# An overflow check behind the output's stores, ranking among the first products, and small experts flipped by transposes

## Chip, cores and metric

The kernel runs on one core of a Trainium2 chip. Its time is the device time of one execution in microseconds; the median of several runs is compared.

## What is computed

A two-layer encoder over 272 tokens (16 meta tokens and 256 of the sequence) of 1024 features. Layer 0 is a convolution module and a dense SwiGLU, layer 1 a pooling mixer and a mixture of experts; each part reads an RMS-normed stream and adds to it, and a last RMS norm follows. The change touches the mixture alone:

```python
def moe_swiglu(h, w_router, e_gate, e_up, e_down):
    logits = (h @ w_router).astype(jnp.float32)
    top_vals, top_idx = lax.top_k(logits, TOP_K)          # 2 of 8
    top_w = jax.nn.softmax(top_vals, axis=-1)
    ...
    for e in range(N_EXPERTS):
        y = y + combine[..., e:e + 1] * swiglu(h, e_gate[e], e_up[e], e_down[e])
```

Each expert's gate, up and down are 1024 x 3584, 1024 x 3584 and 3584 x 1024, all float32.

## The kernel before, in words

The dense layers and the router take the first 385 us. The stage of the experts takes the rest but for the tail. Experts are ranked by how many tokens chose them. Place 0 is expert 0; places 0 to 4 are "big" and hold up to 128 tokens, places 5 to 7 are "small" and hold up to 64. Should an expert have more tokens than its place holds, a body under an `If` (`second_groups`, L1240) computes the rest; on this data it is not entered. Before it, every engine loads the largest count from memory to a register (L1218).

**Steps.** The stage has 56 steps, each one expert and one block of 512 of its 3584 features (7 blocks). From step 7 on small steps stand among the big ones, mostly in turn. A step is three parts on TensorE: `project` for the gate into `pg` (L1155 to L1161), `project` for the up half into `pu`, and `down` for the block of the step before (L1207 to L1210), which adds into sums that stay in PSUM for 7 blocks. In the middle of the gate's project the block of the step before is flipped: its product of gate and up, tokens in partitions, is turned so that features are in partitions. For a big expert `flip` (L1173) does this by four transposes, and ACT and VectorE split the result into a high and a low half. A small expert keeps high and low halves of its 64 tokens side by side in 128 columns, so its halves have to be added as well: `flip_small` makes 16 products (L1190) with a matrix that adds them and scales by the token's norm factor (`factored_sums`), then Silu on ACT, a product (L1194) and the split.

**Weights.** They come as tiles of 1 MB on SP's queue into 15 buffers. Units of 128 x 1024 are split: ACT casts the high half (L104, `W.hi`), VectorE subtracts (L127, `W.lo`), four units ahead of TensorE. When a tile's last unit is read, the next load into its buffer is issued.

**Pieces.** All other work of VectorE and ACT in the stage stands in a list `side`. `beside` is called ten times a step (three in each `project`, four in `down`): it releases casts, takes one piece off the list, and then issues the low halves due. So a piece delays the low halves behind it, by its own time and by what it waits for.

**Start.** After the router VectorE ranks the experts (`places`, L894), reorders positions by place (`by_place`, L918), writes the tokens' factors (`of_tokens`, L927) and weights (`weights_of_tokens`, L935). SP loads the ids of the experts at each place, then the `If` stands, then four loads of the norm's gain on ACT's queue (L1308), and the loop of steps. The first pieces are the factors of expert 0, `rows_of_tokens` (L946), and for each other expert its selection matrix and a small product (`factors`, L1052).

**Sums and rows.** From step 3 on (`SUMS_FROM`) pieces add the high and low halves of the stream into `x_of` (L1336), add that to the accumulator `yacc` (L1352), multiply by the gain (L1341) and write it to memory as `x_rows` (L1342, POOL's queue), for two halves of tokens with one buffer. Each later expert's token rows are fetched from `x_rows` by an indirect DMA on POOL (L1065), one step ahead, and transposed in the up projection of the step ahead of its first. Outputs of all experts but the last are written to memory as `y_rows` and gathered at the end.

**Tail.** The last expert's output is added, the final norm is taken on ACT and VectorE, and four stores on the queues of ACT and SP end the kernel (L1493).

Of the kernel before, what the change touches and what calls it, by code (L numbers as in the profile page):

```python
# [39 lines left out]
ALONE, SUMS_FROM, QUIET = 6, 3, 3  # L40
# [15 lines left out]
class Weights:  # L56


    def __init__(self, nc, raw_pool, hi_pool, lo_pool, tiles):
# [9 lines left out]
        self.held, self.room = None, 0  # L69
# [62 lines left out]
    def read(self, i):  # L132

        self.left[i] -= 1
        if not self.left[i]:
            del self.raw[i]
            self.load(self.home[i])
# [27 lines left out]
def body(tc, xT, w_pw1, w_pw2, w_gu, w_dn, w_pool, m_gate, m_up, m_down, small, moe_g,  # L165
# [108 lines left out]
    twice = consts.tile([128, SMALL_CAP], F32)  # L274
# [619 lines left out]
    def places(scratch):  # L894

        hot, cmp = (squares_of(scratch, i, 1)[:, 0] for i in range(2))
        key, place, most = scratch[:, :NE], scratch[:, NE:NE + n_rest], scratch[:, 2 * NE:2 * NE + 1]
# [12 lines left out]
        DVE.tensor_copy(ids_i, place)  # L910
        DVE.tensor_tensor(cmp, hot, counts[:, None, 1:].to_broadcast(shape), op=OP.mult)
# [66 lines left out]
    yacc = pool(ctx, "yacc").tile([128, 2, D], F32, name="yacc")  # L978
    POOL.memset(yacc, 0.0)
# [14 lines left out]
    def gathered(ps, P, kk, width):  # L994

        for i in range(2):
            n = 0
            for x in (xth, xtl):
                for t in range(2):
# [3 lines left out]
                    n += 1  # L1003

# [11 lines left out]
    class Expert:  # L1016
# [36 lines left out]
        def factors(self):  # L1053

            ps = self.pm.tile([128, 512], F32, name="m")
            for t in range(2):
                PE.matmul(ps[:, :3], lhsT=self.P[:, t].bitcast(F32), rhs=rcq[:, t, self.q],
                          start=(t == 0), stop=(t == 1))
            DVE.tensor_copy(facts[:, self.q], ps[:, :3])
            DVE.tensor_copy(at[:, self.q:self.q + 1], ps[:, 1:2])  # L1060

        def fetch(self, rows):
            n = self.width
            self.rows = rows
            POOL.indirect_dma_start(  # L1065
                out=rows[:n], out_offset=None, in_=x_rows[:, :],
                in_offset=bass.IndirectOffsetOnAxis(ap=at[:n, self.q:self.q + 1], axis=0))
# [55 lines left out]
    with ExitStack() as cs:  # L1123
# [58 lines left out]
        def flip_small(gu, e):  # L1182
# [361 lines left out]
```

## Time and profile before

| | |
|---|---|
| median of 3 runs | 1341.68 us (1340.31 to 1342.72) |
| profiled execution, own time | 1339.14 us |
| its span | 1336.8 us |
| granted TensorE clock, mean | 0.994 |
| PE / DVE / ACT / POOL busy | 97% / 82% / 69% / 2% |
| moved by DMA | 414.21 MB, mean 310 GB/s |

The busy share of an engine is its time in work over the span. A wait is put down to the semaphore that came last; "issue" means that no semaphore shows what the engine waited for. In a timeline several like instructions can share a line with their count, and durations of pipelined instructions overlap, so that the time from start to start is what they take one after another. PEld is the loading of stationary operands, which overlaps products.

### The profile page before, as it was taken

What the parts mean: (1) busy time and instruction counts of PE and PEld (TensorE: products, weight loads), DVE (VectorE), ACT (ScalarE), POOL (GpSimd) and SP (SyncE); (2) the same over time, 40 slices, a digit from 0 to 9 for tenths busy, and PEclk for the clock granted to TensorE, in tenths of its full rate; (3) what the DMA queues carried; (4) which work ended last, traced back from release to release, by engine and by line L of the source; (5) the groups of instructions that cost most, each with busy time, mean ns of one, the idle gap of its engine ahead of it and who ended that gap; (6) DMA issues with size and microseconds to landing.
All of it is one profiled execution on the core that took longest, in us unless ns stands there. A gap on an engine that the chain in (4) does not pass through costs nothing.

```text
span 1336.8 us, 19372 instructions
## 1 busy us (share of the span) xinstructions
PE 1297.4 (97%) x6823; PEld 1055.9 (79%) x6823; DVE 1093.8 (82%) x1435; ACT 918.1 (69%) x1221; POOL 25.8 (2%) x34
## 2 busy tenths in 40 slices
PE   9999999999969899999999999999999999999996
PEld 9989999999957677777777777777777777777775
DVE  7997885666767878888788888888888887888876
ACT  6765643445545568777787777777877776877765
POOL 0000000000000100000000000000000000000010
PEclk9999999999989999999999999999999999999999
DMA  9700446425748899999999699999798999799970
GB/s 367 302 1 1 160 139 223 162 101 189 293 166 318 322 387 372 402 400 400 373 374 395 267 390 421 421 420 421 322 422 331 422 421 421 306 423 420 410 276 31
DMA packets 61783, 414.21 MB, mean 310 GB/s; under 512 B 6896, under 2 KB 8048, under 8 KB 14704
## 3 DMA queue, kind: packets, MB, share of 16 engines
q1 hardware_dynamic: 58032, 402.22, 75.8%
q0 software_dynamic: 1680, 6.03, 1.2%
q10 hardware_dynamic: 1968, 4.66, 1.0%
q8 instruction: 55, 0.90, 0.3%
q14 instruction: 48, 0.39, 0.1%
HBM read 407.90 MB, written 4.98 MB: 309 GB/s over the span
## 4 chain that ended last, share of the span: by engine, by line
PE 62%; DVE 5%; DMA 2%; issue 2%; ACT 1%; ACTq 0%; DVEq 0%
PE pg L1155 10%; PE pu L1155 10%; PE pu L1161 6%; PE pg L1161 6%; PE pyb L1207 4%; PE pyb L1210 4%; PE pyb L1209 4%; PE pg L1159 4%; PE pu L1159 4%; DVE w_lo L127 3%; PE m L1190 3%; PE pys L1207 3%; PE pys L1210 3%; DMA raw<-m_gate 2%; PE m L1173 1%
## 5 line engine op out<-in xcount | busy, mean ns | idle before, releaser
L127 DVE TENSOR_TENSOR w_lo<-raw,w_hi 128x1024 fp32r<-128x1024 f32 (+1 forms) x704 | 821.0, 1204 | 149.2 <-ACT w_hi L104 145.2
L104 ACT CAST w_hi<-raw 128x1024 fp32r<-128x1024 f32 (+1 forms) x704 | 712.7, 1035 | 245.2 <-PE mm L306 68.6
L305 PE MATMUL mm<-xh,w_hi 128*128 128x272 f32 x480 | 139.7, 291 | 0.0
L307 PE MATMUL mm<-xh,w_lo 128*128 128x272 f32 x480 | 139.3, 290 | 0.0
L306 PE MATMUL mm<-xl,w_hi 128*128 128x272 f32 x480 | 138.8, 289 | 0.0
L1207 PE MATMUL pyb<-w_hi,hh 128*128 128x512 f32 x272 | 112.1, 412 | 0.0
L1210 PE MATMUL pyb<-w_lo,hh 128*128 128x512 f32 x272 | 107.7, 396 | 3.9 <-DVE w_lo L127 3.9
L1209 PE MATMUL pyb<-w_hi,hl 128*128 128x512 f32 x272 | 107.3, 395 | 0.0
L306 PEld LDWEIGHTS mm<-xl,w_hi 128*128 128x128 f32 x480 | 90.6, 189 | 0.7 <-DVE xl L322 0.2
L307 PEld LDWEIGHTS mm<-xh,w_lo 128*128 128x128 f32 x480 | 90.4, 188 | 0.5 <-DVE w_lo L374 0.2
L305 PEld LDWEIGHTS mm<-xh,w_hi 128*128 128x128 f32 x480 | 90.5, 188 | 0.1
L1207 PE MATMUL pys<-w_hi,hs 128*128 128x512 f32 x168 | 74.1, 441 | 0.0
L1210 PE MATMUL pys<-w_lo,hs 128*128 128x512 f32 x168 | 66.2, 394 | 0.0
L1210 PEld LDWEIGHTS pyb<-w_lo,hh 128*128 128x128 f32 x272 | 51.2, 188 | 19.0 <-DVE w_lo L127 5.2
L1155 PE MATMUL pu<-raw,x6b 128*128 128x512 f32 x140 | 65.8, 593 | 0.0
L1155 PE MATMUL pg<-raw,x6b 128*128 128x512 f32 x140 | 65.8, 592 | 0.0
L1209 PEld LDWEIGHTS pyb<-w_hi,hl 128*128 128x128 f32 x272 | 51.3, 188 | 13.7 <-issue 2.4
L1207 PEld LDWEIGHTS pyb<-w_hi,hh 128*128 128x128 f32 x272 | 51.2, 188 | 12.8 <-ACT w_hi L104 2.2
L401 DVE SCALAR_TENSOR_TENSOR v<-u,sm,v 128x271 f32<-128x271 f32 (+29 forms) x137 | 55.6, 496 | 0.0
L305 PE MATMUL mm<-gh,w_hi 128*128 128x272 f32 x176 | 50.7, 288 | 0.0
L307 PE MATMUL mm<-gh,w_lo 128*128 128x272 f32 x176 | 50.6, 288 | 0.0
L306 PE MATMUL mm<-gl,w_hi 128*128 128x272 f32 x176 | 50.5, 287 | 0.0
(406 smaller groups left out, 2362.1 us busy)
## 6 DMA issues: line engine op xcount, KB each, us to landing
raw<-m_gate SPq DMA_DIRECT2D x112, 1024.0 KB, 9.5
raw<-m_up SPq DMA_DIRECT2D x112, 1024.0 KB, 11.3
raw<-m_down SPq DMA_DIRECT2D x111, 1024.0 KB, 10.8
raw<-w_gu SPq DMA_DIRECT2D x22, 1024.0 KB, 4.8
raw<-w_dn SPq DMA_DIRECT2D x16, 704.0 KB, 4.0
raw<-w_pw SPq DMA_DIRECT2D x10, 1024.0 KB, 19.2
y_rows<-rows ACTq DMA_DIRECT2D x4, 512.0 KB, 9.5
h<-xT SPq DMA_DIRECT2D x4, 272.0 KB, 4.7
```

Of the source, the lines that this page charges most:

```text
L104: self.nc.scalar.copy(hi[:, :n], self.raw[i][:, s:s + n])
L127: self.nc.vector.tensor_sub(lo, self.raw[i][:, s:s + n], hi.bitcast(F32))
L305: PE.matmul(ps, lhsT=w[0], rhs=x[0], start=first, stop=False)
L306: PE.matmul(ps, lhsT=w[0], rhs=x[1], start=False, stop=False)
L307: PE.matmul(ps, lhsT=w[1], rhs=x[0], start=False, stop=last)
L401: DVE.scalar_tensor_tensor(v[:, c, j:], u[:, c, :T - j], w, v[:, c, j:], op0=OP.mult, op1=OP.add)
L1155: PE.matmul(ps, lhsT=hi, rhs=w[0][:, i], start=(k == 0), stop=(k == KC - 1 and len(w) == 1))
L1159: PE.matmul(ps, lhsT=x[k - i][:, i, n:], rhs=w[0][:, i], start=False, stop=False)
L1161: PE.matmul(ps, lhsT=hi, rhs=w[1][:, i], start=False, stop=(k == KC - 1))
L1207: PE.matmul(ps, lhsT=a, rhs=wh[:, j % 2], start=first, stop=False)
L1209: PE.matmul(ps, lhsT=b[0], rhs=wh[:, j % 2], start=False, stop=False)
L1210: PE.matmul(ps, lhsT=a, rhs=wl[:, j % 2], start=False, stop=last)
```

## The change

1. The `If` and its body move behind the output's stores; the body then takes the norm and stores again. The ids are loaded to SP's registers at step 1, the count to all engines' at step 2.
2. Ranking, the largest count, the order by place and the tokens' weights become pieces of step 0. The copies out of an expert's small product move to the next piece (`known`). `rows_of_tokens` moves to the step of the sums.
3. The gain's four loads go on POOL's queue.
4. `yacc` is no longer a tile of its own, set to zero. Its place holds one more weight tile (`W.once`) until step 4, now `SUMS_FROM`; then the sum of the halves is written into it directly, and the gains multiply from it into `x_of`.
5. Experts 1 and 5 are both fetched at the top of step 5, expert 1 first; expert 5's rows are transposed in the same step.
6. `flip_small` makes eight transposes into two banks; ACT copies one half, VectorE adds the other; Silu, product and split become pieces at the head of the list. The norm factor is applied as `pg` and `pu` are read out. A big flip's low half becomes a piece as well. `factored_sums` goes.
7. The final outputs go to tiles of their own, so that `yacc` stays whole for the body.

In the body, which is not entered, the gathered products are replaced by fetched rows; that part is left out here.

```diff
@@ -37,7 +37,7 @@
 LINE = 16
-ALONE, SUMS_FROM, QUIET = 6, 3, 3
+ALONE, IDS_AT, COUNT_AT, SUMS_FROM, QUIET = 6, 1, 2, 4, 3
@@ -66,7 +66,7 @@
         self.raw, self.home, self.done, self.ahead = {}, {}, {}, W_BUFS
-        self.held, self.room = None, 0
+        self.held, self.once, self.room = None, None, 0
@@ -134,7 +134,8 @@
             del self.raw[i]
-            self.load(self.home[i])
+            if self.home[i] is not self.once:
+                self.load(self.home[i])
@@ -908,6 +908,11 @@
         DVE.tensor_copy(ids_i, place)
+
+    def count_most(scratch):
+        hot, cmp = (squares_of(scratch, i, 1)[:, 0] for i in range(2))
+        most = scratch[:, 0:1]
+        shape = [128, n_rest, n_rest]
@@ -975,8 +980,8 @@
     W.more(pool, ctx, 1)
-    yacc = pool(ctx, "yacc").tile([128, 2, D], F32, name="yacc")
-    POOL.memset(yacc, 0.0)
+    W.once = pool(ctx, "once")
+    W.load(W.once)
@@ -1001,6 +1006,11 @@
                     n += 1
+
+    def fetch_rows(rows, q, n):
+        POOL.indirect_dma_start(
+            out=rows[:n], out_offset=None, in_=x_rows[:, :],
+            in_offset=bass.IndirectOffsetOnAxis(ap=at[:n, q:q + 1], axis=0))
@@ -1050,30 +1060,24 @@
-        def factors(self):
-
-            ps = self.pm.tile([128, 512], F32, name="m")
+        def factors(self, n=3):
+
+            self.f = self.pm.tile([128, 512], F32, name="m")
             for t in range(2):
-                PE.matmul(ps[:, :3], lhsT=self.P[:, t].bitcast(F32), rhs=rcq[:, t, self.q],
-                          start=(t == 0), stop=(t == 1))
-            DVE.tensor_copy(facts[:, self.q], ps[:, :3])
-            DVE.tensor_copy(at[:, self.q:self.q + 1], ps[:, 1:2])
+                PE.matmul(self.f[:, :n], lhsT=self.P[:, t].bitcast(F32),
+                          rhs=rcq[:, t, self.q, :n], start=(t == 0), stop=(t == 1))
+
+        def known(self, n=3):
+            DVE.tensor_copy(facts[:, self.q, :n], self.f[:, :n])
+            DVE.tensor_copy(at[:, self.q:self.q + 1], self.f[:, 1:2])
         def fetch(self, rows):
-            n = self.width
             self.rows = rows
-            POOL.indirect_dma_start(
-                out=rows[:n], out_offset=None, in_=x_rows[:, :],
-                in_offset=bass.IndirectOffsetOnAxis(ap=at[:n, self.q:self.q + 1], axis=0))
+            fetch_rows(rows, self.q, self.width)
...
             gathered_rows(x, self.rows, kk, self.width, self.pm, plain)
-
-        def factored_sums(self):
-
-            self.sums = self.tile([128, SMALL_CAP], F32, "sums")
-            DVE.tensor_scalar(self.sums, twice, self.r, None, op0=OP.mult)
@@ -1179,21 +1183,38 @@
-        def flip_small(gu, e):
+        def turned(ps, h_t, n=4):
+            for j in range(n):
+                PE.transpose(ps[:, j * 128:(j + 1) * 128], h_t[:, j * 128:(j + 1) * 128], ident)
+
+        def flip_later(h_t):
+
+            ps = pm.tile([128, 512], F32, name="m")
+            turned(ps, h_t)
+            hi, lo = flip_tiles()[0]
+            ACT.copy(hi, ps)
+            side.insert(0, lambda: DVE.tensor_sub(lo, ps, hi.bitcast(F32)))
+            return [(hi, lo)]
+
+        def flip_small(gu):
             n = SMALL_CAP
-            ps = pm.tile([128, 512], F32, name="m")
+            v = ws.tile([128, 2, 4, n], F32, name="v", tag="yl", bufs=1)
             for a, t in enumerate(gu):
-                for j in range(4):
-                    c = (a * 4 + j) * n
-                    PE.matmul(ps[:, c:c + n], lhsT=t[:, j * 128:(j + 1) * 128], rhs=e.sums,
-                              start=True, stop=True)
-            v = ws.tile([128, 4 * n], F32, name="v", tag="ut", bufs=1)
-            ACT.activation(v, ps[:, :4 * n], AF.Silu)
-            DVE.tensor_mul(v, ps[:, 4 * n:], v)
+                ps = pm.tile([128, 512], F32, name="m")
+                turned(ps, t)
+                ps = ps.rearrange("p (j c) -> p j c", j=4)
+                ACT.copy(v[:, a], ps[:, :, :n])
+                DVE.tensor_add(v[:, a], ps[:, :, n:], v[:, a])
             t = ws.tile([128, 4, 2 * n], F32R, name="hs", tag="hh", bufs=1)
-            split(t[:, :, :n], t[:, :, n:], v.rearrange("p (j c) -> p j c", j=4))
+
+            def through():
+                DVE.tensor_mul(v[:, 0], v[:, 0], v[:, 1])
+                ACT.copy(t[:, :, :n], v[:, 0])
+
+            side[:0] = [lambda: ACT.activation(v[:, 0], v[:, 0], AF.Silu), through,
+                        lambda: DVE.tensor_sub(t[:, :, n:], v[:, 0], t[:, :, :n].bitcast(F32))]
@@ -1293,33 +1311,34 @@
         scratch = ws.tile([128, 256], F32, name="scratch", tag="PTb", bufs=1)
-        places(scratch)
-        by_place(posq, posm, scratch)
-        for q in range(1, NE):
-            expert_at[q] = nc.values_load(
-                ids_i[0:1, q - 1:q], engines=(mybir.EngineType.SP,), min_val=1, max_val=NE - 1,
-                skip_runtime_bounds_check_because="each is one of experts 1 to 7")
         of_tokens()
-        weights_of_tokens(scratch)
-        second_groups()
...
         for i, t in enumerate(gain1):
-            nc.scalar.dma_start(t, bass.AP(tensor=moe_g.tensor, offset=moe_g.offset + i * 256,
+            nc.gpsimd.dma_start(t, bass.AP(tensor=moe_g.tensor, offset=moe_g.offset + i * 256,
...
         table(AF.Silu)
-        side += [experts[0].factors, lambda: rows_of_tokens(scratch),
-                 lambda: DVE.tensor_add(twice, ident[:, :64], ident[:, 64:128])]
+        side += [lambda: experts[0].factors(2),
+                 lambda: (experts[0].known(2), places(scratch)),
+                 lambda: (count_most(scratch), by_place(posq, posm, scratch)),
+                 lambda: weights_of_tokens(scratch)]
+        before = lambda: None
...
             e = experts[q] = Expert(q, ws, pm)
-            side += [lambda e=e: e.assign(posq), e.factors]
+            side += [lambda e=e, before=before: (before(), e.assign(posq)), e.factors]
+            before = e.known
             if q == BIG - 1:
-                side.append(e.back)
+                before = lambda e=e: (e.known(), e.back())
+        side.append(before)
...
         prev, py_of, n_fetched = None, {}, 0
+
+        def fetch(q):
+            experts[q].fetch(fetched_rows[n_fetched % 2])
+
@@ -1328,17 +1347,25 @@
                     tensor=final_g.tensor, offset=final_g.offset, ap=[[0, 128], [1, D]]))
+            if n_step == IDS_AT:
+                for i in range(1, NE):
+                    expert_at[i] = nc.values_load(
+                        ids_i[0:1, i - 1:i], engines=(mybir.EngineType.SP,), min_val=1,
+                        max_val=NE - 1,
+                        skip_runtime_bounds_check_because="each is one of experts 1 to 7")
+            if n_step == COUNT_AT:
+                count = nc.values_load(cnt_i[0:1, 0:1], min_val=0,
+                                       max_val=SEQ + CAP - SMALL_CAP,
+                                       skip_runtime_bounds_check_because="a count of SEQ tokens")
             if n_step == SUMS_FROM:
+                yacc = W.once.tile([128, 2, D], F32, name="raw")
...
-                def sums_begin(t):
+                def gains(t):
                     x_of[t] = ws.tile([128, D], F32, name="x_of", tag="yh", bufs=1)
-                    DVE.tensor_add(x_of[t], xth[:, t].bitcast(F32), xtl[:, t].bitcast(F32))
-
-                def gains(t):
                     for i, g in enumerate(gain1):
-                        x = x_of[t][:, i * 256:(i + 1) * 256]
-                        DVE.tensor_mul(x, x, g)
+                        c = slice(i * 256, (i + 1) * 256)
+                        DVE.tensor_mul(x_of[t][:, c], yacc[:, t, c], g)
@@ -1348,10 +1375,11 @@
                 for t in range(2):
-                    pieces += [lambda t=t: sums_begin(t),
-                               lambda t=t: DVE.tensor_add(yacc[:, t], x_of[t], yacc[:, t]),
+                    pieces += [lambda t=t: DVE.tensor_add(yacc[:, t], xth[:, t].bitcast(F32),
+                                                          xtl[:, t].bitcast(F32)),
                                lambda t=t: gains(t)]
-                side[:0] = pieces + [freed]
+                temp = ws.tile([128, 256], F32, name="scratch", tag="ut", bufs=1)
+                side[:0] = pieces + [freed, lambda: rows_of_tokens(temp)]
@@ -1373,10 +1401,11 @@
-            if n_step + 1 in after_of:
-                new = after_of[n_step + 1]
-                assert n_step > SUMS_FROM
-                experts[new].fetch(fetched_rows[n_fetched % 2])
+            if n_step + 1 in after_of and n_step > SUMS_FROM:
+                fetch(after_of[n_step + 1])
+                n_fetched += 1
+            if n_step in after_of and n_step - 1 <= SUMS_FROM:
+                fetch(after_of[n_step])
@@ -1388,15 +1417,13 @@
                     t, p = prev[0], prev[1]
-                    hT.append(flip_small(t, p) if p.small else flip(t, flip_tiles()))
+                    hT.append(flip_small(t) if p.small else flip_later(t))
...
                 ht = [ws.tile([128, 512], F32, name=n, bufs=1) for n in ("ht", "ut")]
-                ACT.copy(ht[0], pg)
-                if f == 0:
-                    e.factored_sums()
+                ACT.activation(ht[0], pg, AF.Copy, scale=e.r)
@@ -1405,7 +1432,7 @@
             if e.small:
-                ACT.copy(ht[1], pu)
+                ACT.activation(ht[1], pu, AF.Copy, scale=e.r)
@@ -1429,7 +1456,6 @@
         r = ws.tile([128, 2], F32, name="r", bufs=1)
-        junk = ws.tile([128, 512], F32, name="junk", tag="ht", bufs=1)
@@ -1444,14 +1470,15 @@
-        def squares(s, t):
+        def squares(junk, s, t):
...
-        o = [ws.tile([128, 512], F32, name="o", tag=k, bufs=1) for k in ("x4b", "ut")]
+        o = [[ws.tile([128, 512], F32, name="o", tag=k, bufs=1), own_rows[t][:, :512]]
+             for t, k in enumerate(("x4b", "ut"))]
         def gained(t):
-            POOL.tensor_mul(o[t], yacc[:, t, cols[0]], gain[:, :512])
+            POOL.tensor_mul(o[t][0], yacc[:, t, cols[0]], gain[:, :512])
@@ -1474,23 +1501,29 @@
         put(1)
-        for t in range(2):
-            gained(t)
-            squares(0, t)
-        for t in range(2):
-            add(1, t)
-            squares(1, t)
-        DVE.tensor_add(sq[:, 0], sq[:, 0], sq[:, 1])
-        rsqrt(r, sq[:, 0], 0, ws, 2)
-        for t in range(2):
-            for s in range(2):
-                y, f = yacc[:, t, cols[s]], r[:, t:t + 1]
-                if s == 0:
-                    y = o[t]
-                    ACT.activation(y, y, AF.Copy, scale=f)
-                else:
-                    DVE.scalar_tensor_tensor(y, y, f, gain[:, 512:D], op0=OP.mult, op1=OP.mult)
-                (nc.scalar, nc.sync)[s].dma_start(out[t * 128:(t + 1) * 128, cols[s]], y)
+
+        def norm_and_store(add=lambda s, t: None):
+            junk = ws.tile([128, 512], F32, name="junk", tag="ht", bufs=1)
+            for t in range(2):
+                gained(t)
+                squares(junk, 0, t)
+            for t in range(2):
+                add(1, t)
+                squares(junk, 1, t)
+            DVE.tensor_add(sq[:, 0], sq[:, 0], sq[:, 1])
+            rsqrt(r, sq[:, 0], 0, ws, 2)
+            for t in range(2):
+                for s in range(2):
+                    y, f = o[t][s], r[:, t:t + 1]
+                    if s == 0:
+                        ACT.activation(y, y, AF.Copy, scale=f)
+                    else:
+                        DVE.scalar_tensor_tensor(y, yacc[:, t, cols[1]], f, gain[:, 512:D],
+                                                 op0=OP.mult, op1=OP.mult)
+                    (nc.scalar, nc.sync)[s].dma_start(out[t * 128:(t + 1) * 128, cols[s]], y)
+
+        norm_and_store(add)
+        second_groups(count)
...

```

## Rows read from the trace of the kernel before

**Rows 1.** PE's waits: engine, tile, line, releaser: us in total, times, longest

```profile
PE pu L1161 <- DVE w_lo L127: 9.8, 19, 0.7
PE pg L1155 <- issue: 9.7, 1, 9.7
PE pyb L1210 <- DVE w_lo L127: 3.9, 3, 2.5
```

**Rows 2.** Line 1240, the If: durations ns min/median/max, first and last start

```profile
L1240 PEldq COMPARE_BRANCH  x2: 95/1994/3894, 380.8 to 381.1; - x2
```

**Rows 3.** Line 1218, the load of the count, on PE's queue

```profile
L1218 PEldq TENSOR_LOAD <-cnt_i x1: 492/492/492, 380.2 to 380.2; - x1
```

**Rows 4.** Timeline 377 to 386, PE and ACT: start us, us, instruction, [idle before]

```profile
377.73 0.20 ACT L885 ACTIVATE ex<-dl 128x2 f32<-128x2 f32 x1 [0.30 <-DVE dl L884]
...
385.20 0.76 PE L1155 MATMUL pg<-w_hi,x0b 128*128 128x512 f32 x1 [9.73 <-issue]
...
385.49 1.28 ACT L282 ACT_TABLE_LOAD   x1 [7.55 <-DMA gain<-moe_g]
```

**Rows 5.** Timeline 377 to 384, DVE

```profile
377.61 0.16 DVE L899 SCALAR_TENSOR_TENSOR scratch<-counts,slots 128x8 f32<-128x8 f32 x1
...
380.64 0.17 DVE L930 COPY rcq<-rst 128x8 f32<-128x8 f32 x1
...
380.93 0.16 DVE L937 TENSOR_SCALAR den<-ex 128x2 f32<-128x2 f32 x1
...
382.80 0.16 DVE L925 COPY rcq<-rc 128x2 f32<-128x2 f32 x1
```

**Rows 6.** Windows: us, PE, PEld, DVE, ACT, POOL busy, PEclk, DMA share, GB/s

```profile
385.20:399.52 14.32, 14.32 (x52) 10.70 (x53) 9.51 (x29) 8.46 (x9) 0.00 (x0) 0.85 0.62 197
438.35:460.89 22.54, 18.63 (x73) 12.98 (x72) 17.92 (x23) 11.67 (x13) 1.32 (x2) 1.00 0.82 300
460.89:479.12 18.23, 18.10 (x74) 13.13 (x72) 15.26 (x15) 11.68 (x13) 5.77 (x2) 1.00 0.97 348
563.30:580.62 17.32, 17.32 (x78) 13.09 (x77) 13.14 (x14) 11.59 (x13) 0.00 (x0) 1.00 0.99 393
580.62:595.07 14.45, 13.92 (x62) 10.64 (x60) 14.45 (x14) 13.39 (x17) 0.00 (x0) 1.00 1.01 408
825.00:857.00 32.00, 31.47 (x139) 23.90 (x138) 27.89 (x28) 25.22 (x29) 0.00 (x0) 1.00 1.01 421
```

**Rows 7.** Timeline 566 to 583, PE: a small and a big expert's flip

```profile
566.09 1.00 PE L1190 MATMUL m<-sumss,ht 128*128 128x64 f32 x8
...
567.79 0.48 PE L1155 MATMUL pg<-w_hi,x4b 128*128 128x512 f32 x1
...
582.48 0.60 PE L1173 MATMUL m<-iw,ht 128*128 128x128 f32 x4
582.83 0.48 PE L1155 MATMUL pg<-w_hi,x4s 128*128 128x512 f32 x1
```

**Rows 8.** Groups by line and form, 470 to 1300 us

```profile
L127 DVE TENSOR_TENSOR w_lo<-raw,w_hi 128x1024 fp32r<-128x1024 f32 x548 | 644.1, 1222 | 112.5 <-ACT w_hi L104 110.3
...
L1194 DVE TENSOR_TENSOR v<-m,v 128x256 f32<-128x256 f32 x21 | 8.9, 425 | 1.4
```

**Rows 9.** Timeline 440 to 470, POOL

```profile
447.42 0.77 POOL L1342 DMA_DIRECT2D x_rows<-x_of  x1 [78.67 <-DVE x_of L1341]
...
463.80 4.30 POOL L1065 DMA_INDIRECT rows<-x_rows,at  x1 [4.26 <-DMA x_rows<-x_of]
468.41 1.47 POOL L1065 DMA_INDIRECT rows<-x_rows,at  x1 [0.30 <-issue]
```

**Rows 10.** Timeline 438 to 462, DVE: the sum that waits

```profile
452.69 1.23 DVE L1336 TENSOR_TENSOR x_of<-xth,xtl 128x1024 f32<-128x1024 f32 x1 [4.45 <-DMA x_rows<-x_of]
```

**Rows 11.** Line 1065, the indirect fetches: from issue to landing

```profile
DMA to landing us min/median/max: 7.5/9.7/11.7
```

**Rows 12.** Timeline 1325 to 1340, the last issue on ACT's queue

```profile
1332.60 0.34 ACTq L1493 DMA_DIRECT2D out<-o  x1
```

More of the change, by code (lines that the diff above doesn't have):

```diff
@@ L273, in body @@
     wr = dconsts.tile([128, KC, NE], F32)
-    twice = consts.tile([128, SMALL_CAP], F32)
     token = consts.tile([128, LINE], F32)
@@ L896, in places @@
         hot, cmp = (squares_of(scratch, i, 1)[:, 0] for i in range(2))
-        key, place, most = scratch[:, :NE], scratch[:, NE:NE + n_rest], scratch[:, 2 * NE:2 * NE + 1]
+        key, place = scratch[:, :NE], scratch[:, NE:NE + n_rest]
         shape = [128, n_rest, n_rest]
@@ L1214, in down, with second_groups @@
                     beside()
-        def second_groups():
-            count = nc.values_load(cnt_i[0:1, 0:1], min_val=0, max_val=SEQ + CAP - SMALL_CAP,
-                                   skip_runtime_bounds_check_because="a count of the SEQ tokens")
+        def second_groups(count):
             hT = flip_tiles()
-            x = {kk: ws.tile([128, 2, 128], F32, name="x", tag="x%ds" % kk, bufs=1)
-                 for kk in range(0, KC, 2)}
-            w = ws.tile([128, 2, 512], F32, name="w", tag="yh", bufs=1)
-            ht = ws.tile([128, 512], F32, name="ut", bufs=1)
+            tile = raw_pool.tile([128, RAW], F32, name="raw")
+            x = tile[:, :1024].rearrange("p (k s) -> p k s", k=KC)
+            w = tile[:, 1024:].rearrange("p (n c) -> p n c", n=2)
+            ht = ws.tile([128, 512], F32, name="ht", bufs=1)
             cr = ws.tile([128, LINE], F32, name="cr2", bufs=1)[:, :3]
-            PT = hT[0][0][:, :256]
             P = ws.tile([128, 2, 128], F32R, name="P", bufs=2)
+            PT = ws.tile([128, 256], F32R, name="PT", tag="PTb", bufs=1)
             pg, pu = [p.tile([128, 512], F32, name=n) for p, n in ((pg_pool, "pg"), (pu_pool, "pu"))]
@@ L1242, in second_groups @@
                     assign(P, q, CAP if q < BIG else SMALL_CAP, 128, posq)
-                    for kk in range(0, KC, 2):
-                        ps = pm.tile([128, 512], F32, name="m")
-                        gathered(ps, P, kk, 128)
-                        for i in range(2):
-                            ACT.activation(x[kk][:, i], ps[:, i * 128:(i + 1) * 128], AF.Copy,
-                                           scale=g1[:, kk + i:kk + i + 1])
                     ps = pm.tile([128, 512], F32, name="m")
@@ L1253, in second_groups @@
                     DVE.tensor_copy(cr, ps[:, :3])
+                    DVE.tensor_copy(at[:, q:q + 1], ps[:, 1:2])
+                    fetch_rows(fetched_rows[0], q, 128)
+                    for kk in range(0, KC, 2):
+                        gathered_rows(x[:, kk:kk + 2], fetched_rows[0], kk, 128, pm, True)
                     for f in range(FT):
@@ L1257, in second_groups @@
                                 p, i = divmod(k, KC // 2)
-                                products(ps, [x[k - k % 2][:, k % 2]],
+                                products(ps, [x[:, k]],
                                          tile_of(src, q, f, p)[:, i * 512:(i + 1) * 512],
@@ L1274, in second_groups @@
                     for s in range(2):
-                        weigh(s, ("ht", "yl"))
+                        weigh(s)
                         for t in range(2):
@@ L1280, in second_groups @@
                             DVE.tensor_add(y, ps, y)
+                norm_and_store()
         experts = {0: Expert(0, ws, pm)}
```

## The prediction

> **What bounds the kernel now.** I read the page's busy shares first (TensorE 97%), then the view of waits, to see what the missing 3% is, and then windows cut at the steps of the expert stage, since a share of the whole span says nothing about one step. The waits of TensorE [rows 1] have one big entry: 9.7 us once, before the first gate product of the stage, released by "issue", which means no semaphore of a tile. The other two entries are waits for the low halves of weights, short ones of 0.7 us at most and one of 2.5 us.
>
> The 9.7 us is the overflow test. TensorE idles until 385.20, for 9.73 us [rows 4]; at 380.2 it loads the count [rows 3], then takes the branch, 3894 ns [rows 2]. Before that it waits while VectorE ranks the experts: the ranking begins at 377.61, the tokens' factors follow at 380.64, the weights at 380.93, and the last copy is at 382.80 [rows 5].
>
> The windows [rows 6] show the steps. Step 0 lasts 14.32 us at a granted clock of 0.85, so 2.1 us of it is clock that the idle stretch cost. Step 3, with the sums and gains, lasts 22.54 us with 18.63 us of TensorE work; step 4 after it takes 18.23. Later a big step after a small one takes 17.32 us with TensorE busy for all of it and VectorE for 13.14; a small step after a big one takes 14.45 us with VectorE busy for all of it. So a big step is TensorE's and a small one VectorE's, and which step an instruction stands in decides what it costs.
>
> **The change part by part.** The sum is made against the profiled execution's own 1339.14 us; the median of the runs shown, 1341.68, lies 2.5 above it, and I add that at the end.
>
> *The start.* Without the branch TensorE can begin step 0 at about 376.0 in place of 385.20: 9.2 gained, and some 0.9 of the 2.1 lost to the clock, as the idle stretch is shorter (a guess between 0 and 2.1). But ranking, count and weights now stand between the low halves of step 0. Exp ends at 377.93 and the table for Silu takes 1.28 [rows 4]; the first cast ends near 380.5 and the first low halves follow. Up to expert 1's selection VectorE then has two times four low halves, which follow each other in about 1.15 us (1.22 us each with the overlap [rows 8]), 9.2 us; ranking with the count 3.0 (377.61 to 380.64) and weights 2.0 [rows 5], of which about 1.0 falls after that point or overlaps; together about 10.3, so 390.8. TensorE needs it for the factors behind the up projection's last piece, at about 387.1. It waits 3.7. Sum: -9.2 - 0.9 + 3.7 = **-6.4**. Ends: -11 if TensorE does not wait there, -2 if the clock gives nothing back and the wait is twice as long.
>
> *The count and the ids.* TensorE's load of the count takes 492 ns [rows 3] and now stands ahead of step 2's products: **+0.5**. SP's loads of ids are ahead of weight loads, but tiles are well ahead at that point: 0.
>
> *Gain's loads on POOL* instead of ACT: POOL's next work is at 447.42, after 78.67 us of idle [rows 9]; 0. ACT's queue loses four issues, hidden too.
>
> *Sums and gains.* In step 3 VectorE sat 4.45 us until the first half of x_rows had landed, since the second half's sum wanted the same buffer [rows 10]. Now the sum goes into the weight buffer, and two adds of 1.22 are gone; the second half's gains still write that buffer, but three operations of 1.15 stand in between. Of the 22.54, 4.7 goes against a step of 17.8; step 4, which gets the pieces and what is left of the wait (about 4.45 - 2.3 = 2 us on VectorE, mostly under its lead of four units), pays 0.6 (0 to 3): **-4.1**.
>
> *Fetched rows in step 5.* Before, expert 5's rows were asked for in step 4, at 463.80; that first indirect DMA held POOL 4.30 us, and expert 1's followed at 468.41 [rows 9]. Landing takes 7.5 to 11.7 us [rows 11]. Now both are asked for at the top of step 5, expert 1's first, and expert 5's rows are transposed by TensorE in that same step. If the first again takes 4.3 us, expert 5's is issued 4.6 us into the step and lands at 12.1 to 16.3; the first transpose is due about 8 us in (behind the fourth of the step's ten pieces of 1.8 us, and the flip). TensorE waits 4.1 to 8.3; I take 6, and 2 for the clock: after the pause of 9.7 it averaged 0.85 over a step, and the rows have no pause between that and 2.5 [rows 1, 6]. **+8** (0 to 11).
>
> *Flips of the small experts.* The 16 products with the sums matrix take 566.09 to 567.79, 1.70 us; a big expert's four transposes take 582.48 to 582.83, 0.35, and their starts lie 0.109 apart [rows 7]. Eight transposes are then 0.35 + 4 x 0.109 = 0.79. 0.91 saved each, 21 times, and all of them fall in big steps, where TensorE has no idle time: **-19.1**. The added work (two adds of 128x256, by the row of the product 0.425 us each [rows 8], and two copies on ACT, with scaled evictions) is some 0.85 per pair on VectorE and 1.0 on ACT. It stands in the big step, whose 17.32 hold 13.14 of VectorE and 11.59 of ACT; so 0. If that cover were gone, it would cost what rival three says. The deferred low half of a big flip keeps VectorE's order: 0.
>
> A rule of the Trainium skill speaks against this part. By the rows a transpose takes 0.109 us start to start, so the part gains. "TensorE: Matmul & The Clock Gate", Part 4 (PE-mode transpose), gives about 275 ns for one transpose in the context of a kernel; if they queued at that rate, eight would be an estimated 2.2 us and the part would lose 0.5 each time. In [rows 7] four take 0.35 in all; the trace does not agree, and I take the rows.
>
> *The end.* The branch moves behind the output's stores. The last store issues at 1332.60 and the span ends at 1336.8 [rows 12]. If every engine must wait for the stores before it jumps, the jump comes on top. Bounds: 0 (it runs under the stores) and 3.9 (TensorE's branch [rows 2]), more if the engines meet first. I take 2.7 plus eight semaphore steps, **+3.3**, near the upper end because the jump is to code that has not been run, as at the start.
>
> In "Advanced Engine Details and Errata", Control Flow Timing, the Trainium skill gives about 108 ns for a compare-and-branch; by that the end would be nearly free. The row of 3894 ns here disagrees, and I go by the row.
>
> Sum: -6.4 + 0.5 - 4.1 + 8 - 19.1 + 3.3 = -17.8: own time 1321.3, and with the 2.5 **1324 us**.
>
> **The rivals.** *Rows in time.* If the first indirect DMA is short (the second took 1.47 [rows 9]) or the transposes come late enough, the +8 falls away: 1316. For it: the 4.30 may be a first use that a shorter queue shortens. Against: landing alone takes 7.5. Chance 0.25.
>
> *The weight stream binds.* A pair of steps moves 17.32 x 393 + 14.45 x 408 = 12.7 MB [rows 6]. At 400 GB/s that is 31.8 us, the pair's time now; then the flips gain nothing, and 1324 + 19 = 1343, about no change with the start's gains against step 5's and the end's cost; I say 1341. Against: 421 GB/s in 825 to 857 [rows 6], at which a pair needs 30.2, under the 30.9 that I forecast. Chance 0.06.
>
> *Slower: the added work lands where VectorE is full.* If the adds, or the pieces that they push, fall into the small step, its 14.45 are VectorE's and each pair pays. The point is the 4.1 us of VectorE's idle time in a big step (17.32 - 13.14): once the late low halves of the big step reach into the small one, 0.85 + 0.91 per pair is lost against my sum: 21 x 1.76 = 37, **1361**. For it: VectorE is busy for the whole small step. Against: the pieces are put ahead of the others at the top of the big step. Chance 0.05.
>
> *Slower: transposes at their full duration.* If eight queue at 0.27 us each, the flips cost 0.5 x 21 = 10.5 instead of gaining 19.1: **1354**. Against: 0.109 apart in [rows 7]. Chance 0.03.
>
> The rest, **0.61**, is my forecast; the start's and the end's bounds lie within it.
>
> **How the numbers follow.** About 0.2%, 2.7 us, is what a measurement of this kernel can tell from no change. 1324 is the likeliest case. Its own bounds (start -4.6 to +4.4, rows -8 to +3, end -3.3 to +0.6, step 4 up to +2.4), which will not all fall together, give about 1314 to 1334; with the case of rows in time that is 1312 to 1335, and both slower rivals and the stream stay out with 0.14. Faster by over 0.2% means below 1339: the forecast and rows in time, 0.86; same is the stream, 0.06; slower the last two, 0.08.
>
> **What would show it.** Right: no wait by "issue" on the first gate product, and one for VectorE in step 0 of some 4 us; steps 3 and 4 of 17.8 and 18.8; a wait of TensorE on the fetched rows in step 5; eight transposes within 0.8 us and big steps after small ones of 16.4; the last stores followed by a few us. Wrong: big steps still 17.3 with waits for low halves or for raw tiles; small steps longer than 14.5; step 5 without a stall, or one over 12.

## The result, and the profile after

The changed kernel takes 1323.49 us (median of 4 runs, 1321.8 to 1330.13) against 1342.03 before: a ratio of 0.9872, 95% interval 0.9855 to 0.9889. The forecast was 1324. The profiled execution takes 1321.80 (span 1319.8) against 1339.14 (1336.8), and the two traces can be laid side by side by the first gate product of each step. The total fits better than its parts:

| stretch | forecast | before to after, in the traces |
|---|---|---|
| up to step 1 | -6.4 | 399.52 to 394.27: -5.25 |
| steps 1 and 2 | +0.5 | +0.61 and +0.45: +1.06 |
| steps 3 and 4 | -4.1 | 40.77 to 37.46: -3.31 |
| step 5 | +8 | 19.66 to 23.78: +4.12 |
| steps 6 to 54 | -19.1 | -18.46 |
| last step to the last store's issue | 0 | +0.99 |
| from there to the end of the span | +3.3 | 3.9 to 7.7: +3.8 |
| sum | -17.8 | -17.0 |

The windows of the changed kernel, cut as in [rows 6]: steps 0, 4 and 5, a big step after a small one, a small one after a big one, and the last step up to TensorE's last product.

```profile
376.22:394.27 18.05, 14.69 (x53) 9.91 (x53) 13.54 (x49) 9.76 (x12) 0.00 (x0) 0.87 0.60 224
451.99:471.62 19.63, 18.09 (x74) 13.16 (x72) 15.80 (x24) 11.68 (x13) 1.08 (x2) 1.00 0.83 306
471.62:495.40 23.78, 21.46 (x81) 14.74 (x80) 18.16 (x30) 12.40 (x17) 2.96 (x2) 0.93 0.98 369
558.94:575.33 16.39, 16.39 (x70) 12.15 (x68) 13.49 (x16) 11.95 (x15) 0.00 (x0) 1.00 1.02 423
575.33:589.84 14.51, 13.97 (x62) 10.66 (x61) 14.51 (x14) 13.54 (x17) 0.00 (x0) 1.00 1.01 420
1277.30:1306.29 28.99, 27.76 (x129) 20.21 (x127) 23.60 (x25) 16.89 (x23) 2.18 (x2) 1.00 0.05 20
```

The fourth and fifth lines answer to 17.32 and 14.45 in [rows 6]: 0.93 less in the big step, still TensorE's alone, and 0.06 more in the small one, still VectorE's alone. VectorE's work in the big step rose from 13.14 to 13.49 only, so the two adds found room in its idle time. The stream carried 423 and 420 GB/s, with the DMA engines' share at 1.02 and 1.01 (the last two columns), so little room is left there; but TensorE in the one step and VectorE in the other have no idle time in which they could wait for weights, so it did not bind.

A small expert's flip in TensorE's timeline, to be read against [rows 7]:

```profile
561.74 0.60 PE L1188 MATMUL m<-iw,ht 128*128 128x128 f32 x4
562.18 0.60 PE L1188 MATMUL m<-iw,ut 128*128 128x128 f32 x4
562.53 0.48 PE L1159 MATMUL pg<-w_hi,x4b 128*128 128x512 f32 x1
```

561.74 to 562.53 is 0.79 for eight transposes, the forecast's figure.

TensorE's waits of the changed kernel (L1165 and L1231 are L1161 and L1210 of before):

```profile
PE pu L1165 <- DVE w_lo L127: 9.9, 19, 0.7
PE m L1067 <- DVE P L997: 3.1, 1, 3.1
PE pg L1165 <- DVE w_lo L127: 2.3, 1, 2.3
...
PE pyb L1231 <- DVE w_lo L127: 1.5, 1, 1.5
```

The 9.7 us by "issue" of [rows 1] are gone. In their place stands the wait for expert 1's selection in step 0, 3.1 us. The stall of step 3 has not gone but moved: 1.5 us at the end of step 4 and 2.3 at the top of step 5, where [rows 1] had 3.9 in three. No wait for fetched rows is listed.

What held the low halves is in VectorE's timeline, the line that answers to [rows 10]:

```profile
466.57 1.43 DVE L1368 TENSOR_TENSOR x_of<-raw,gain 128x256 f32<-128x256 f32 x4 [3.55 <-DMA x_rows<-x_of]
```

3.55 us in place of 4.45: the second half's gains still want the buffer that the first half's store reads. That store landed later than before. These are the landing times of the two stores of x_rows, before and after; the first store has the longer time in both:

```profile
DMA to landing us min/median/max: 4.0/4.6/5.2
DMA to landing us min/median/max: 2.9/5.6/8.3
```

Behind the gains VectorE then ranks the rows (`rows_of_tokens`, from L962 on), 2.4 us in which no low half is made:

```profile
470.86 0.16 DVE L962 TENSOR_SCALAR scratch<-place_of 128x8 f32<-128x8 f32 x1
...
473.28 2.35 DVE L127 TENSOR_TENSOR w_lo<-raw,w_hi 128x1024 fp32r<-128x1024 f32 x2
```

Three windows show what the wait in step 0 and the two waits around 470 did to the clock:

```profile
389.00:391.00 2.00, 0.38 (x2) 0.38 (x3) 2.00 (x6) 0.00 (x0) 0.00 (x0) 0.66 0.45 188
391.00:396.00 5.00, 5.00 (x10) 2.74 (x11) 2.73 (x4) 0.00 (x0) 0.00 (x0) 0.50 0.62 210
474.00:478.00 4.00, 3.44 (x9) 2.73 (x10) 4.00 (x5) 1.04 (x1) 1.30 (x1) 0.62 1.00 408
```

After 3.1 us of waiting in step 0 the granted clock is 0.50 (1.2 GHz) for all of 391 to 396, which costs 2.5 us more, and after the two waits around 470 it drops once more. Step 0 in VectorE's timeline: what it does in front of expert 1's selection (L997).

```profile
380.60 1.23 DVE L127 TENSOR_TENSOR w_lo<-raw,w_hi 128x1024 fp32r<-128x1024 f32 x1 [2.41 <-ACT w_hi L104]
...
383.46 1.23 DVE L127 TENSOR_TENSOR w_lo<-raw,w_hi 128x1024 fp32r<-128x1024 f32 x1
...
386.08 1.22 DVE L127 TENSOR_TENSOR w_lo<-raw,w_hi 128x1024 fp32r<-128x1024 f32 x1
...
389.15 1.22 DVE L127 TENSOR_TENSOR w_lo<-raw,w_hi 128x1024 fp32r<-128x1024 f32 x1
390.29 0.48 DVE L997 TENSOR_SCALAR P<-slots,posq 128x128 fp32r<-128x128 f32 x2
```

The load of the count on TensorE's queue, and TensorE's timeline around it:

```profile
L1357 PEldq TENSOR_LOAD <-cnt_i x1: 488/488/488, 413.0 to 413.0; - x1
```

```profile
412.90 0.39 PE L1228 MATMUL pyb<-w_hi,hh 128*128 128x512 f32 x1
413.13 0.39 PE L1230 MATMUL pyb<-w_hi,hl 128*128 128x512 f32 x1
413.36 0.40 PE L1231 MATMUL pyb<-w_lo,hh 128*128 128x512 f32 x1
413.60 0.51 PE L1067 MATMUL m<-rcq,P 128*128 128x3 f32 x4
```

POOL's timeline, to be read against [rows 9], and the landing of [rows 11]:

```profile
472.03 1.02 POOL L1011 DMA_INDIRECT rows<-x_rows,at  x1 [3.20 <-PE pyb L1231]
473.35 1.94 POOL L1011 DMA_INDIRECT rows<-x_rows,at  x1 [0.30 <-issue]
```

```profile
DMA to landing us min/median/max: 8.3/8.9/11.0
```

Both fetches start within the first 2 us of step 5, and the first holds POOL for 1.02 where 4.30 was reckoned with. Expert 5's rows, fetched second, have landed at 482.3. TensorE, late by its own stall, comes to them at 483.6, 12 us into the step, and finds them there.

The end: the last store's issue, then the test's line on the queues of SP and TensorE, then the first of SP's closing waits.

```profile
1311.67 0.42 ACTq L1523 DMA_DIRECT2D out<-o  x1
```

```profile
L1259 SPq EVENT_SEMAPHORE  x8: 17/17/17, 1312.2 to 1315.6; - x8
...
L1259 PEldq COMPARE_BRANCH  x2: 95/1696/3297, 1305.6 to 1306.5; - x2
...
L1259 SPq COMPARE_BRANCH  x2: 38/46/53, 1312.1 to 1315.7; - x2
```

```profile
L1573 SPq EVENT_SEMAPHORE  x14: 17/28/28, 1318.1 to 1319.7; - x14
```

SP goes through eight semaphores until 1315.6, when the stores have landed (the last at 1315.4), branches at 1315.7, and its next instruction starts at 1318.1: 2.4 us of jump that nothing covers. TensorE's own branch, 3.3 us, was over long before. The Trainium skill, "Runtime: NRT & Kernel Launch", Instruction fetch mechanics, says that a taken branch may have to fetch its target before execution goes on; the 2.4 us behind a branch of at most 0.05 agree with that.

### The profile page after: what moved, and what is told of

The parts are those of the page before. It is cut to its first block, busy times and chain, and to the rows that moved or that the text cites. A ratio compares the mean times of both kernels' runs of the same rounds, so it can differ in the third digit from the quotient of the medians.

```text
span 1319.8 us, 19130 instructions
## 1 busy us (share of the span) xinstructions
PE 1281.9 (97%) x6655; PEld 1037.6 (79%) x6655; DVE 1099.2 (83%) x1471; ACT 928.5 (70%) x1263; POOL 21.8 (2%) x37
## 4 chain that ended last, share of the span: by engine, by line
PE 85%; DVE 8%; issue 4%; ACT 1%; DMA 1%; DVEq 0%; ACTq 0%
PE pu L1159 10%; PE pg L1159 9%; PE mm L307 7%; PE mm L306 7%; PE mm L305 7%; PE pu L1165 6%; DVE w_lo L127 6%; PE pyb L1228 5%; PE pyb L1231 5%; PE pyb L1230 5%; PE pg L1165 5%; PE pg L1163 4%; PE mm L507 4%; PE pu L1163 3%; PE pys L1231 2%
## 5 line engine op out<-in xcount | busy, mean ns | idle before, releaser
L1231 PE MATMUL pyb<-w_lo,hh 128*128 128x512 f32 x272 | 107.5, 395 | 1.5 <-DVE w_lo L127 1.5
L1231 PE MATMUL pys<-w_lo,hs 128*128 128x512 f32 x168 | 66.3, 395 | 0.0
L1231 PEld LDWEIGHTS pyb<-w_lo,hh 128*128 128x128 f32 x272 | 51.2, 188 | 15.8 <-DVE w_lo L127 2.0
```

The source lines that it names most:

```text
L1231: PE.matmul(ps, lhsT=a, rhs=wl[:, j % 2], start=False, stop=last)
```

## The experiments

Times are medians; ratios are to the kernel before on the same chip. The ratio of the changed kernel is 0.9872.

**The flips alone**, put into the kernel before with all that point 6 of the change names; the line that calls them:

```diff
-                    hT.append(flip_small(t, p) if p.small else flip(t, flip_tiles()))
+                    hT.append(flip_small(t) if p.small else flip_later(t))
```

> The kernel before with the new flips alone (eight transposes, halves added by ScalarE and VectorE, the rest of both flips as pieces). Theory: they are the whole gain; a big step after a small one goes from 17.3 to 16.4, a small step gains 0.03: 21 x 0.88 = 18.5, so 1342.0 - 18.5 = 1323.5, the time of the changed kernel. Rival: the rest of the change gains as well, at its start above all, and the flips alone give 1329 or more.

1321.97 us, 0.9870 (0.9851 to 0.9890): the whole gain, and all else that was changed sums to nothing that can be measured, within the width of the two intervals, some 3 us. In its trace steps 6 to 54 take 18.8 less than before, against 18.5 in the changed kernel. A pair of its steps reads as in the changed kernel:

```profile
562.22:578.60 16.38, 16.38 (x69) 12.14 (x68) 13.52 (x16) 11.94 (x15) 0.00 (x0) 1.00 1.01 422
578.60:593.12 14.52, 13.99 (x62) 10.67 (x60) 14.52 (x14) 13.53 (x17) 0.00 (x0) 1.00 1.02 421
```

**Does it matter that the rest of the flips are pieces?** Silu, product and split of a small flip, and the low half of a big one, at once behind the transposes:

```diff
-            side.insert(0, lambda: DVE.tensor_sub(lo, ps, hi.bitcast(F32)))
+            DVE.tensor_sub(lo, ps, hi.bitcast(F32))
...
-            side[:0] = [lambda: ACT.activation(v[:, 0], v[:, 0], AF.Silu), through,
-                        lambda: DVE.tensor_sub(t[:, :, n:], v[:, 0], t[:, :, :n].bitcast(F32))]
+            ACT.activation(v[:, 0], v[:, 0], AF.Silu)
+            through()
+            DVE.tensor_sub(t[:, :, n:], v[:, 0], t[:, :, :n].bitcast(F32))
```

> The changed kernel with Silu, product and split issued right behind the transposes and not as pieces. Theory: VectorE has 2.9 us of idle time in a big step (16.39 less 13.5), and its waits for ScalarE in the chain stay under that: within 3 us of 1323.5. Rival: the chain holds the low halves behind it back, and TensorE waits for them in each big step after a small one, by the 0.9 that the flips gained or more: 1342 or more.

1324.44 us, 0.9893 (0.9864 to 0.9922), and a big step after a small one still lasts 16.40. So VectorE's slack covers the chain either way in the steady steps. In steps 4 and 5, where VectorE is behind, its trace has 46.51 in place of 43.41, with 2.6 us of waiting for fetched rows; two of its six runs took over 1332, and why is open. One more thing differed that was not expected: the last step took 28.06 in place of 28.99.

**What the branch at the start was worth**: the kernel before without it.

```diff
-        second_groups()
```

> The kernel before without its If and the body (which this data does not enter), and without the load of the count. Theory: ranking and weights hold the first low halves until about 384 anyway, so the branch alone is worth little: 1 to 3 us, 1339 to 1341, and TensorE waits for low halves at the top of step 0. Rival: the branch is all of the 9.7 us that TensorE waited: 1342.0 - 9 = 1333.

1338.89 us against 1340.84; the ratio, 0.9997 (0.9981 to 1.0012), does not tell it from no change. In its profiled execution step 1 starts at 396.45, 3.1 earlier. The 9 of the rival is excluded. The wait stands elsewhere than expected, before the product of expert 0's factors:

```profile
383.12 1.01 PE L1057 MATMUL m<-rcq,P 128*128 128x3 f32 x4 [5.34 <-DVE rcq L925]
```

VectorE's ranking, with the weights behind it, holds TensorE for 5.3 of the 9.7 us even without a branch. So the gain at the start needed the ranking spread as well.

**What the branch at the end costs**: the changed kernel without it.

```diff
         norm_and_store(add)
-        second_groups(count)
```

> The changed kernel without the If at the end and its body (which this data does not enter). Theory: the branch is paid in full, since SyncE jumps only when the stores have landed. From the last issue to the end of the span the kernel before takes 3.9 us and the changed one 7.7; the 3.8 go away, so 1323.5 - 3.8 = 1319.7. Rival one, the branch lies under the landing: no change, 1323.5. Rival two, part of the 3.8 are slower stores (landing 3.5 us in place of 2.8): 3.1 go away, 1320.4.

1318.7 us, 0.9830 (0.9816 to 0.9845). In its trace the span ends 4.0 us after the last store's issue, against 7.7: nearer to the theory's 3.8 than to the 3.1 of slower stores. The rest of the 4.8 between the medians is no part of the end.

**The wait in step 0.** Five empty pieces stand in front of expert 1's selection, so that TensorE comes to the product that needs it later in its own order:

```diff
+        side += [lambda: None] * 5
         before = lambda: None
```

> The changed kernel with five empty pieces between the tokens' weights and expert 1's selection. Theory: TensorE's wait of 3.12 us for the selection in step 0 goes, and with it the clock of 0.50 from about 390 to 396, which costs 3.0: 1323.5 - 6.1 = 1317.4, with steps 0 and 1 near 14.9 and 20.2. Rival: VectorE is behind by the ranking whatever comes next, and a wait for low halves takes the place of the one removed: at most 1 us gained, 1322.5 or more.

1319.05 us, 0.9841 (0.9817 to 0.9866). Step 0 runs at full clock and step 1 starts 5.9 sooner. Part of that is only moved: step 2 takes 1.2 more with the small products that now stand in it (16 in place of 8), so step 3 starts 4.9 sooner.

```profile
375.90:388.33 12.43, 12.19 (x48) 8.58 (x49) 9.20 (x42) 9.75 (x12) 0.00 (x0) 1.00 0.55 207
```

That is more than the wait of 3.1 us: the clock behind it was to be had as well.

**The waits around step 5.** First a second buffer for x_of, so that VectorE need not wait:

```diff
-                    x_of[t] = ws.tile([128, D], F32, name="x_of", tag="yh", bufs=1)
+                    if t:
+                        freed()
+                    x_of[t] = own_rows[1] if t else ws.tile([128, D], F32, name="x_of", tag="yh",
+                                                            bufs=1)
...
-                side[:0] = pieces + [freed, lambda: rows_of_tokens(temp)]
+                side[:0] = pieces + [lambda: rows_of_tokens(temp)]
```

> The changed kernel with a second buffer for the second half of x_of. Theory: VectorE's wait of 3.55 us for the landing of x_rows in step 4 is what makes TensorE wait 1.54 us there and 2.32 us at the top of step 5, and the low clock after that costs 2.0 more: all 5.9 go away, 1317.6, steps 4 and 5 near 18.1 and 19.8. Rival: the ranking of rows that stands behind it (2.4 us of VectorE) is enough by itself for the second wait and the clock: 1.5 go away, 1322.

1325.51 us, 0.9888 (0.9872 to 0.9904): no gain, and both theories fell. Steps 4 and 5 take 18.16 and 27.30. The waits for low halves are gone, and the next thing is late:

```profile
PE m L1019 <- DMA rows<-x_rows,at: 4.7, 1, 4.7
```

That is the wait on expert 5's rows that the forecast had named; the stall in front of it had hidden it. Step 5 with it is 7.6 longer than in the kernel before (19.66), at a granted clock of 0.87:

```profile
469.52:496.82 27.30, 22.44 (x82) 15.25 (x81) 16.19 (x19) 12.52 (x17) 2.88 (x2) 0.87 0.88 326
```

The other half of the same pair, the ranking of rows taken to step 6:

```diff
+                side[:0] = pieces + [freed]
+            if n_step == 6:
                 temp = ws.tile([128, 256], F32, name="scratch", tag="ut", bufs=1)
-                side[:0] = pieces + [freed, lambda: rows_of_tokens(temp)]
+                side.append(lambda: rows_of_tokens(temp))
```

> The changed kernel with the ranking of rows moved from step 4 to step 6. Theory (the wait for x_rows is the cause and the ranking of rows adds to it): the wait of 1.54 us in step 4 stays, the one of 2.32 in step 5 goes or nearly so, and with it the low clock: 1323.5 - 4.3 = 1319.2. Rival (the wait for x_rows alone is enough): under 1 us, 1322.5 or more.

1330.74 us (1330.56 to 1331.31), 0.9922 (0.9909 to 0.9936): slower by 7. Of the two waits for low halves the one at the top of step 5 is gone, as its theory had it, and 1.2 us in step 4 are left; so it took the ranking of rows to make the second. But TensorE waited 10.7 us on the fetched rows, and POOL's timeline shows why it was so much longer here:

```profile
472.48 6.61 POOL L1011 DMA_INDIRECT rows<-x_rows,at  x1 [3.20 <-PE pyb L1231]
479.39 1.32 POOL L1011 DMA_INDIRECT rows<-x_rows,at  x1 [0.31 <-issue]
```

The first indirect DMA held POOL for 6.61 us, where the changed kernel has 1.02, and expert 5's is second. All three edits together:

> The changed kernel with the second buffer, the five empty pieces and the ranking of rows in step 6. Theory: the waits and the low clock of steps 0, 4 and 5 go together, 6.1 and 5.9: 1323.5 - 12.0 = 1311.5. Rival: the steps are then bound by VectorE's backlog and the gains don't add up: 1316 or more.

1321.49 us, 0.9853 (0.9839 to 0.9866). The empty pieces' gain is there, but step 5 takes 28.29, with 6.3 us on the rows: the theory's sum fell for the same reason.

**A new theory**: two waits in a row, low halves first and rows behind them. So the sums go back to step 3, which puts expert 5's fetch a step ahead of its use; alone, and with the second buffer and the empty pieces.

```diff
-ALONE, IDS_AT, COUNT_AT, SUMS_FROM, QUIET = 6, 1, 2, 4, 3
+ALONE, IDS_AT, COUNT_AT, SUMS_FROM, QUIET = 6, 1, 2, 3, 3
```

> The changed kernel with the sums from step 3 on, and nothing else changed. Theory: the wait for x_rows stays and stalls TensorE by 3 to 4 us in step 3 or 4, with the low clock after it, but the rows of expert 5 can no longer be late: the median stays at 1322 to 1324, and no run is near 1330. Rival: the sums in step 3 do not disturb, since two adds are gone: 1318 or less.

1321.41 us, 0.9846 (0.9811 to 0.9881): 0.6 under what was expected and above the rival's 1318, with waits of 1.5 and 2.3 us a step earlier. But one run took 1329.73. In the profiled execution both fetches have landed by 464.6, 19 us ahead of the first use, so late rows hardly make a single run of this kernel that long; of the long run itself there is no trace, and its cause stays open.

> The changed kernel with the sums from step 3 on, so that expert 5's rows are fetched at step 4, a step ahead of their use; the second buffer for x_of; and the five empty pieces in step 0. Theory: steps 4 and 5 were slow by two things in a row, the wait for x_rows and, once that is gone, the rows of expert 5, asked for in the step that uses them. Both go: steps 3 to 5 near 18.2, 18.1 and 19.7, 56.0 in place of 61.3; with the 4.9 of the empty pieces 1323.5 - 5.3 - 4.9 = 1313.3. Rival: the waits only move to step 3 or 4 again, and it is no better than the empty pieces alone, 1318 or more.

1312.66 us, 0.9784 (0.9751 to 0.9818), and steps 3 to 5 sum to the 56.0 that were expected:

```profile
430.17:448.33 18.16, 18.08 (x73) 13.12 (x72) 17.33 (x37) 11.68 (x13) 1.08 (x2) 1.00 0.74 277
448.33:466.55 18.22, 18.09 (x74) 13.14 (x72) 15.26 (x15) 11.68 (x13) 4.71 (x2) 1.00 0.97 355
466.55:486.20 19.65, 19.65 (x82) 13.66 (x80) 14.31 (x17) 12.43 (x17) 0.94 (x1) 1.00 1.01 413
```

> As e9_sums_sooner_all with three empty pieces in place of five and the ranking of rows in step 6. Theory: TensorE waits about 1 us more for the selection in step 0, and the ranking of rows is no longer on VectorE's path with the sums; the two differ by less than 2 us: 1311 to 1315. Rival: any pause in step 0 brings the low clock: 1316 or more.

1312.28 us, 0.9767 (0.9738 to 0.9796), within 1 us of the former; two fewer empty pieces do no harm. The wait of 1 us that the theory expected did not come (step 0 takes 12.43 with three pieces as with five), so what a short pause there does to the clock stays untested.

**The last step**, with its big flip split at once:

```diff
-                    hT.append(flip_small(t) if p.small else flip_later(t))
+                    hT.append(flip_small(t) if p.small else flip(t, flip_tiles()) if last else
+                              flip_later(t))
```

> As e11_gap3_rows6, with the big flip of the last step split at once, as in the kernel before. Theory: in the last step the flip's piece pushes the gathered sums one place back, and the low halves of the last product come late by it; the last step goes from 29.0 to 28.1 and the kernel from 1312.3 to 1311.4. Rival: the last step is longer for another reason: 29.0 and 1312.3.

1310.63 us, 0.9750 (0.9722 to 0.9777). The difference to the former is under what two medians can tell, but the step itself is 28.05 in place of 29.01:

```profile
1266.62:1294.67 28.05, 27.48 (x129) 20.29 (x127) 23.48 (x25) 16.89 (x23) 2.17 (x2) 1.00 0.08 31
```

This version is faster than both kernels and keeps the overflow test.

## Why the prediction was right, point by point

*Flips, right.* 0.91 per flip, 21 times, was the forecast: the 21 steps that hold a small expert's flip are 0.88 to 0.94 shorter, 19.1 in all. The other steps from 6 to 54 pay 0.6 together, and the last step 0.92 that the forecast had at nothing, for the low half of a big flip as a piece. The rule of the Trainium skill ("TensorE: Matmul & The Clock Gate", Part 4) would have made them a loss; the trace disagrees for this use: 0.79 for eight. The rivals of the stream and of work that lands in the small steps did not come.

*Start: the number met, the working not.* Expert 1's selection was forecast ready at 390.8, and the product that needs it starts at 390.62; the wait is 3.1 for 3.7. But the terms of that forecast, 9.2 and 3.0 and all but 1.0 of 2.0, sum to 13.2 and not to 10.3; with them the selection would have come at 393.7. In the trace four low halves stand in front of it and not eight, 4.6 us, with 3.1 of ranking and count and 1.9 of weights: the hit is luck. The clock term was wrong in sign: the 0.9 that it was to give back was lost instead. The new wait brought the low clock again, which costs at least 2.5 where it cost 2.1 before; step 0 has 0.87, and step 1, with the tail, 0.95. The empty pieces show wait and clock together: 4.9 sooner at step 3.

*Count: the number met, the reason not.* Step 2 is longer by 0.45, where 0.5 was forecast for TensorE's load. But the load stands at 413.0, in step 1, and the products around it start 0.23 apart without a gap. Step 2 is longer because it holds eight of the small products where it held four before; with the flips at once it holds four again and takes 18.30, against 18.28 before, with the same load ahead of it.

*Sums and gains: the step that failed.* "-4.1" took the stall for gone but for 2 us under VectorE's lead. Step 3 came out as forecast, 17.83, but VectorE waited 3.55 in step 4 in place of 4.45. It had 4.0 us more of other work between the first store's issue and that wait than before, but the store landed 8.3 us after its issue in place of 5.2. The forecast had taken the landing as it was. In the traces of the changed kernel and of all that were made from it this landing takes 7.6 to 8.5, in those of the kernel before and of the two made from it 3.9 to 5.2; why was not tried. And the ranking of rows, 2.4 us of VectorE right behind the gains, had no price in the forecast. So TensorE's stall moved whole into steps 4 and 5, with the low clock behind it in step 5.

*Fetched rows: right in price, wrong in place.* +8 was the price of a wait that the changed kernel does not show, as the moved stall stands in front of it; step 5 pays 4.12 for the stall. With the stall removed the wait comes at once, 4.7 and 6.3 us, and with a long first indirect DMA 10.7; the 4.7 with the low clock made step 5 7.6 longer than before, close to the 8, though the first indirect DMA held POOL for 1.02 there and not for 4.30. That the rows are in time was a rival at 1316; they were, but its time did not come, since what made them so was another stall.

*End, right:* +3.8 for +3.3, between the bounds, and paid by SP rather than TensorE: its jump is 2.4, where 2.7 was taken.

So the total was met partly by luck. By cause, the sums and gains came out at +0.8 for -4.1, which is 4.9 worse, and the rows at nothing for +8. All else together was 3.8 worse: the start 1.15, steps 1 and 2 0.56, steps 6 to 54 0.64, the last step 0.99, the end 0.5. These errors cancelled but for 0.8. What is not luck is the flips: they alone make the whole gain.

## What to carry to other kernels

When a stall goes, ask what stands next in the same queue before booking its time: here low halves hid late rows, and removing one alone gained nothing. Taking a branch away from an idle engine gains only what nothing else holds back: without the branch, the ranking still held TensorE for 5.3 of the 9.7 us. A test that is moved behind the stores costs its jump there, 2.4 us here. When a DMA's landing is part of a sum, allow for it to change with the kernel around it. What runs in the steady steps, 21 times 0.9 us, outweighed all the moves at the edges.

## What was not expected of the hardware

A pause of TensorE of 3.1 us was followed by a granted clock of 0.50 for 391 to 396, so that it cost nearly twice its length; waits of 1.5 and 2.3 us around 470 were followed by 0.62 in 474 to 478, while the waits of step 3 in the kernel before, 2.5 us the longest, left the window at 1.00 [rows 6]. The issue of the first indirect DMA on POOL took 4.30 us before [rows 9], 1.02 in the changed kernel and 6.61 with the ranking of rows moved; over all traces it lies between 0.94 and 6.61, and what sets it was not tried. The store of the first half of x_rows landed 8.3 us after its issue in the changed kernel and 5.2 before.
